# Decode attention with gate over sum applied to its outputs, and fifteen loads moved to ACT's queue

## Chip, core and metric

One core of a Trainium2 chip runs the whole step in one launch. The metric is device time in microseconds. TensorE is called PE below, VectorE DVE, ScalarE ACT, GpSimd POOL and SyncE SP; SP issues most of the DMAs and does no arithmetic.

## What is computed

One inference step of a decoder layer, on 1024 prompt positions and on 8 decode sequences of 4 new positions each, all in float32. The input projection gives queries, keys and values of three attention branches, a retention group and gates; attention and retention feed the output projection, and a convolutional feed-forward network (FFN) follows. What the change touches is the attention of the decode sequences, three softmaxes whose outputs are summed by gates:

```python
s_c = jnp.einsum('bqgrd,bcgd->bgrqc', qg, kc) * scale
p_c = jnp.where(m_c, jax.nn.softmax(jnp.where(m_c, s_c, NEG), axis=-1), 0.0)
o_cmp = jnp.einsum('bgrqc,bcgd->bqgrd', p_c, vc)
...
p_s = jax.nn.softmax(s_s, axis=-1).reshape(B, NSA_KV, NSA_REP, Qn, k_top, SEL_BLOCK)
o_sel = jnp.einsum('bgrqkl,bgqkld->bqgrd', p_s, vs)
...
p_w = jax.nn.softmax(jnp.where(m_w, s_w, NEG), axis=-1)
o_win = jnp.einsum('bgrqw,bwgd->bqgrd', p_w, vw.astype(F32))
out = g[..., 0:1] * o_cmp + g[..., 1:2] * o_sel + g[..., 2:3] * o_win
```

The keys and values of the selected branch come from a paged cache: 8 pages of 128 rows for each sequence, gathered by a page table.

## The kernel before

**Stages.** The input projection runs over six groups of weight columns; the decode caches' compressed keys are made beside the first four. `run(4, ...)` projects the attention queries and `run(5, ...)` the retention gates (`ret_gate`, a Silu on ACT at L299); the decode attention (`decode_phase`) runs beside both, as a generator that `run` advances by a few steps for each row tile. In the trace `run(5, ...)` lies at about 340 to 411 us. Then comes the prompt's attention (to 860), with the rest of the decode attention in its first 140 us, the output projection woven into it, and the FFN (888 to the end).

**Weights.** Each weight column group comes in four slices of 512 KB (`w_raw(u)`, u = 0 to 23). A slice lands in one of two raw buffers, `RAW[u % 2]`, and `w_split(u)` turns it into a high and a low part: `wh` by ACT (L186) and `wl` by DVE (L187). The load of slice u + 2 is issued when slice u is split. A projection takes three matmuls for each pair of slice part and row tile (L235, L237, L238; L240 for the decode rows), on `xt` and `xa`, the row tiles' high and low parts.

**Decode attention.** Four rounds, B = 0 to 3, of two sequences each. A round first computes the compressed branch (L709 is its exp, L718 and L722 two small matmuls that rank the blocks), then the window branch (keys `gw`, 512 wide) and then the selected branch (pages `ga`, 1024 wide). `probabilities` (L742) makes a softmax: two exps on ACT (L748: 64 x 512 or 64 x 1024, and 64 x 32 for the new keys) with their sums, the sum's reciprocal times the gate on DVE (L749 to L751), and both blocks of exps multiplied by that on DVE (L753). PE transposes the result (L763), ACT copies it out of PSUM (L764), and PE multiplies it with the values (L779 pages or window, L786 new keys, L784 compressed keys) into one bank, `XB`. The window branch's sum waits in `of` until the selected branch's is added to it.

**Pages.** `load_page` reads a page number into a register of SP and issues the page's load (L463, 128 KB). `run` calls it up to `PG` = 3 times for each row tile; the selected branch issues what is left over.

**Prompt keys and values.** `load_kv` reads the prompt's keys (4 loads of 256 KB, into the two raw buffers) and later its values (4 loads, into `VT`) back from the output in HBM. They, the masks' constants (`hn`, `fin`, `cmpm`) and the last weights are issued by SP (`D` is SP's queue, `S` is ACT, `V` DVE, `T` PE, `G` POOL).

**Order.** A scheduler sets the order on each engine when the kernel is built, by the dependences and priorities of the code; the decode generator's steps have a raised priority. Each engine works its list in order, and so does each queue.

```python
def probabilities(src, n, z, gate):
    s, r, m = [sc[:, 8 + y:9 + y] for y in range(2)], sc[:, 10:11], sc[:, 11:12]
    V.tensor_reduce(m, NM[:, 0:z + 1], AX.X, ALU.min)
    for y, (o, a) in enumerate(((P[:64, 0:n], src), (pn, pn))):
        S.activation(o, a, AF.Exp, bias=m, accum_out=s[y])
```

Of the kernel before, what the change touches and what calls it, by code (L numbers as in the profile page):

```python
# [11 lines left out]
ALU = mybir.AluOpType  # L12
# [47 lines left out]
def hymba(ctx: ExitStack, tc: tile.TileContext, A, O):  # L60
# [99 lines left out]
    def w_raw(u, ks=(0, 2)):  # L160

        c, q = divmod(u, 4)
        if u < 24:
            n = CH_N[c]
            o = 8 * CH_OFF[c] + q * 2 * n
            a, b = ks[0] * n, ks[1] * n
            D.dma_start(raw_ap(u)[:, a:b], A["w_in"][:, o + a:o + b])

    def raw_ap(u):
        return (RAW[u % 2] if u not in (2, 3) else QBIG[:, 1024 + u * 1024:2048 + u * 1024])[:, 0:2 * CH_N[u // 4]]  # L170
# [452 lines left out]
    def decode_phase():  # L623
# [14 lines left out]
            return DCT[:p, o:o + s]  # L638

        of = QBIG[:64, 4608:4736]  # L640
        pc = QBIG[:64, 5120:5248]
        pct, pn = sm[:, 0:64], sm[:, 64:96]
        imr, im, eq, dn = sm[:, 96:113], sm[:, 113:130], sm[:, 130:144], sm[:, 144:160]
        grow = sm[:, 176:188].rearrange("p (b c) -> p b c", c=3)
# [56 lines left out]
        def compressed(B):  # L701

            scc = t_bank()[:64, 0:64]
            for b in range(2):
                scores(scc, KCD[:, B * 128 + b * 64:B * 128 + b * 64 + 64], b)
            nm, s1, r1 = sc[:, 0:1], sc[:, 1:2], sc[:, 2:3]
            V.tensor_reduce(nm, scc[:, 0:63], AX.X, ALU.max, negate=True)
            V.memset(pc[:, 63:64], 0.0)
            S.activation(pc[:, 0:63], scc[:, 0:63], AF.Exp, bias=nm, accum_out=s1)  # L709
            V.reciprocal(r1, s1)  # L710
            V.tensor_scalar(pc[:, 0:63], pc[:, 0:63], r1, None, ALU.mult)
            yield
            tb = t_bank()
            T.transpose(tb[0:64, 0:64], pc[:, 0:64], ident[:64, :64])
            V.tensor_copy(pct, tb[0:64, 0:64])
            yield
            tb = t_bank()
            T.matmul(tb[0:64, 0:17], pct, dc("ovl"), start=True, stop=True)  # L718
            V.tensor_copy(imr, tb[0:64, 0:17])
            yield  # L720
            tb = t_bank()
            T.matmul(tb[0:64, 0:17], dc("rsum"), imr, start=True, stop=True)  # L722
            V.tensor_copy(im, tb[0:64, 0:17])
            mn, mx = sc[:, 3:4], sc[:, 4:5]
            jv = dc("jv")
            V.tensor_reduce(mn, im[:, 1:15], AX.X, ALU.min)
            V.scalar_tensor_tensor(eq, im[:, 1:15], mn, jv[:, 1:15], ALU.is_equal, ALU.mult)
            V.tensor_reduce(mx, eq, AX.X, ALU.max)
            V.tensor_scalar(dn, jv, mx, NEG, ALU.is_equal, ALU.mult)
            V.tensor_scalar(pc[:, 0:64], pc[:, 0:64], grow[:, B, 0:1], None, ALU.mult)  # L730
            V.tensor_copy(pc[:, 64:128], pc[:, 0:64])
            yield

        NM = sc[:, 5:8]
# [7 lines left out]

        def probabilities(src, n, z, gate):

            s, r, m = [sc[:, 8 + y:9 + y] for y in range(2)], sc[:, 10:11], sc[:, 11:12]
            V.tensor_reduce(m, NM[:, 0:z + 1], AX.X, ALU.min)
            for y, (o, a) in enumerate(((P[:64, 0:n], src), (pn, pn))):
                S.activation(o, a, AF.Exp, bias=m, accum_out=s[y])  # L748
            V.tensor_tensor(s[0], s[0], s[1], ALU.add)  # L749
            V.reciprocal(r, s[0])  # L750
            V.tensor_tensor(r, r, gate, ALU.mult)  # L751
            for a in (P[:64, 0:n], pn):
                V.tensor_scalar(a, a, r, None, ALU.mult)  # L753

        def key_scores(src, b):

# [14 lines left out]
        def out(b):  # L771
            return XB[32 * b:32 * b + 32, 0:128]
# [7 lines left out]

        def last_values(br, B):
            for b in range(2):
                if not br:
                    T.matmul(out(b), PD[:, 9, b], VCD[:, B], start=False, stop=False)  # L784
            for b in range(2):
                T.matmul(out(b), PD[0:32, 8, b], VN[:, br], start=False, stop=True)  # L786

        def window_branch(B):
            gw = [GW[:, b * 1024:(b + 1) * 1024] for b in range(2)]
# [10 lines left out]
            last_values(1, B)  # L800
            window(B + 1)
            yield
            V.tensor_copy(of, XB[:64, 0:128])

        def selected_branch(B):
            while pages:
# [11 lines left out]
            yield  # L818
            yield from transposed(8)
            tb = t_bank()[:, 0:64]  # L820
            T.transpose(tb, pc, ident[:64, :64])
            for b in range(2):
                q = slice(64 * b, 64 * b + 64)
                V.tensor_copy(PD[q, 9, b], tb[q, b * 32:(b + 1) * 32])
# [1 line left out]
            for hf in range(2):  # L826
# [3 lines left out]
                    for b in range(2):  # L830
                        gather(B + 1, b)
                yield
            V.tensor_tensor(of, XB[:64, 0:128], of, ALU.add)
            tb = t_bank()[:, 0:64]
            T.transpose(tb, of, ident[:64, :64])
            for z in range(2):
# [112 lines left out]
    pr.release()  # L949
    side = decode_phase()  # L950
    next(side)
    run(4, q_proj, staged, down, side, SB[0], 3)
    KT = pa_.tile([128, 8 * HALF], F32R, name="kt", tag="a0")[:, 0:4096].rearrange("p (b g t) -> p b g t", b=2, g=2)
    VT = []
# [3 lines left out]
    def load_kv():  # L958

        src = O["kv"][0:1024, 256:768].rearrange("(i p) (b z c) -> p i b z c", p=128, b=2, z=2)  # L960
        for y in range(2):
            for b in range(2):
                if VT:
                    D.dma_start(VT[0][:, 4 * y:4 * y + 4, b], src[:, 4 * y:4 * y + 4, b, 1])
                else:
                    D.dma_start(RAW[y].rearrange("p (i b c) -> p i b c", i=4, b=2)[:, :, b], src[:, 4 * y:4 * y + 4, b, 0])

    def masks():
        lt["a"] = kcv.tile([128, 352], F32R, name="ma", tag="ws1")
# [16 lines left out]
    def building(f, order):  # L986

        for z, i in enumerate(order):
            f(i, i == order[-1])
            if z == 1:  # L990
                section("MC", HN[:, 0:MC.size])
                load_kv()
            elif z == 3:
                masks()
# [181 lines left out]
    lt["mo"] = mk(p2, "mo", 128, F32R)  # L1176
    lt["cmpm"] = mk(p2, "cmpm", 120)
    o, _ = SECT["MC"]
    D.dma_start(FIN[:, 0:128], A["const"][:, o + 128:o + 256])
    D.dma_start(lt["cmpm"], A["const"][:, o + 256:o + 376])  # L1180
    V.tensor_copy(lt["mo"], FIN[:, 0:128])
    del ring[:]

# [666 lines left out]
```

## Time and profile before

| what | us |
|---|---|
| median of 3 runs | 1547.77 (1543.68 to 1548.29) |
| profiled execution, its own time | 1553.57 |
| its span, first to last instruction | 1551.8 |
| PE busy in the span | 1488.8 (96%) |
| DVE, ACT, POOL busy | 981.9, 649.8, 617.1 |
| mean TensorE clock granted | 0.976 of full speed |

The trace is that of the profiled execution, so its own time is the one to set sums against. A row of PE's list gives start, length and instruction, and in brackets how long PE had been idle before it and what ended the wait. The clock column of a stretch is the granted TensorE clock as a share of 2.4 GHz: 0.50 is the lower level, 1.2 GHz, and 0.57 is a stretch that is mostly there. Matmuls overlap, so their spacing tells more than their length.

### The profile page before, as it was taken

To read this page: it belongs to the slowest core of one execution; us is meant where nothing else is said; L and a number is where in the kernel's file an instruction comes from. 1 tells how busy PE (TensorE), PEld (TensorE's weight loads), DVE (VectorE), ACT (ScalarE), POOL (GpSimd) and SP (SyncE) were. 2 spreads that over 40 slices of the span, in tenths; PEclk is the share of its full clock that TensorE was granted. 3 is DMA by queue.
4 is the path that set the end of the run, shared out by engine and by line. 5 is a ranking of instruction groups with operands and counts; after the bars stand their busy time and mean duration, and the time that the engine had idled before them with its cause. 6 is when DMAs were issued, how large, how long until landed. Compare 5 with 4: busy or idle time off the path is not lost.

```text
span 1551.8 us, 28741 instructions
## 1 busy us (share of the span) xinstructions
PE 1488.8 (96%) x10722; PEld 1306.8 (84%) x10722; DVE 981.9 (63%) x1831; ACT 649.8 (42%) x1417; POOL 617.1 (40%) x789
## 2 busy tenths in 40 slices
PE   7999999989999789999999899999999999999998
PEld 5898877757656568787877899999999999999998
DVE  6876525364567664645567888777778777644531
ACT  6464324124445554455445433333333334544430
POOL 3453311350224464545345233333333333544552
PEclk8999999998999899999999899999999999999999
DMA  7452301163431100100002124555554535887662
GB/s 265 145 171 63 96 4 55 31 202 95 149 99 59 55 15 28 31 29 28 28 28 69 65 104 156 163 164 167 172 178 165 170 117 168 274 258 220 206 199 66
DMA packets 129568, 184.54 MB, mean 119 GB/s; under 512 B 20356, under 2 KB 89092, under 8 KB 129428
## 3 DMA queue, kind: packets, MB, share of 16 engines
q1 hardware_dynamic: 127940, 178.08, 36.2%
q0 software_dynamic: 1488, 4.63, 0.9%
q8 instruction: 84, 1.38, 0.4%
q14 instruction: 56, 0.46, 0.1%
HBM read 132.84 MB, written 49.82 MB: 118 GB/s over the span
## 4 chain that ended last, share of the span: by engine, by line
PE 82%; DVE 7%; issue 4%; DMA 2%; POOL 2%; ACT 2%; SPq 1%; DVEq 0%; ACTq 0%; POOLq 0%
PE PS L466 51%; PE PS L235 6%; PE PS L238 5%; PE PS L237 5%; PE PS L1103 3%; PE PS L1241 2%; PE PS L1240 2%; PE PS L1242 2%; POOL pwin L1091 1%; PE PS L779 1%; DVE live L1077 1%; DMA raw<-in_w_in 1%; DVE pt L1109 1%; DMA rbig<-in_xT 1%; PE PS L240 1%
## 5 line engine op out<-in xcount | busy, mean ns | idle before, releaser
L466 PE MATMUL PS<-x,wop 128*128 128x264 f32 x3696 | 457.7, 287 | 7.2 <-ACT wop L122 2.9
L466 PEld LDWEIGHTS PS<-x,wop 128*128 128x128 f32 x3696 | 455.7, 190 | 8.9 <-ACT wop L122 3.1
L466 PE MATMUL PS<-h,wop 128*128 128x264 f32 x1848 | 225.6, 285 | 0.0
L466 PEld LDWEIGHTS PS<-h,wop 128*128 128x128 f32 x1848 | 225.4, 188 | 0.0
L123 POOL TENSOR_TENSOR wop<-sp,wop 128x512 fp32r<-128x512 f32 (+1 forms) x105 | 140.0, 1339 | 182.4 <-ACT wop L122 169.1
L122 ACT ACTIVATE wop<-sp 128x512 fp32r<-128x512 f32 x150 | 90.1, 608 | 205.5 <-PE PS L466 105.4
L123 POOL TENSOR_TENSOR wop<-rawf,wop 128x512 fp32r<-128x512 f32 x42 | 70.9, 1689 | 124.3 <-ACT wop L122 124.2
L1077 DVE TENSOR_REDUCE live<-PS 128x1 f32<-128x640 f32 (+5 forms) x112 | 72.0, 652 | 59.8 <-PE PS L466 47.4
L466 PE MATMUL PS<-kt,qt 128*128 128x320 f32 (+5 forms) x400 | 102.0, 351 | 4.8 <-ACT vt L1079 3.9
L1085 POOL TENSOR_TENSOR live<-live 128x2 f32<-128x2 f32 (+1 forms) x64 | 14.5, 227 | 226.2 <-DVE live L1084 203.8
L235 PE MATMUL PS<-wh,xt 128*128 128x512 f32 (+1 forms) x240 | 94.3, 394 | 10.2 <-ACT xt L122 7.3
L466 PE MATMUL PS<-pt,vt 128*64 128x256 f32 x528 | 80.8, 413 | 6.2 <-DVE pt L1109 4.3
L1109 DVE COPY pt<-PS 128x512 f32<-128x512 f32 (+1 forms) x99 | 66.9, 685 | 30.7 <-PE PS L1103 28.4
L1079 ACT ACTIVATE pwin<-PS,live 128x64 f32<-128x64 f32 (+5 forms) x128 | 61.5, 485 | 58.7 <-DVE live L1077 41.9
L1091 POOL TENSOR_TENSOR pwin<-pwin,live 128x64 f32<-128x64 f32 (+5 forms) x128 | 79.1, 649 | 2.2
L238 PE MATMUL PS<-wh,xt 128*128 128x512 f32 (+1 forms) x192 | 75.3, 393 | 2.8 <-DVE xt L123 2.8
L1240 PE MATMUL PS<-mix,wo 128*128 128x256 f32 (+1 forms) x256 | 75.9, 297 | 1.2 <-ACT mix L122 1.1
L123 DVE TENSOR_TENSOR h<-rawf,h 128x528 fp32r<-128x528 f32 x51 | 44.5, 880 | 51.0 <-ACT h L122 50.7
L235 PE MATMUL PS<-wh,xa 128*128 128x512 f32 (+1 forms) x192 | 75.3, 393 | 1.0 <-ACT qbig L253 0.5
L237 PE MATMUL PS<-wl,xt 128*128 128x512 f32 (+1 forms) x192 | 75.5, 394 | 0.0
L466 PEld LDWEIGHTS PS<-kt,qt 128*128 128x128 f32 x400 | 63.7, 197 | 13.1 <-ACT vt L1079 5.1
L1241 PE MATMUL PS<-mix,wo 128*128 128x256 f32 (+1 forms) x256 | 74.1, 290 | 0.5 <-DVE mix L123 0.5
(388 smaller groups left out, 3082.0 us busy)
## 6 DMA issues: line engine op xcount, KB each, us to landing
rawf<-in_w_ffn_in SPq DMA_DIRECT2D x30, 512.0 KB, 3.3
rawf<-scr_x SPq DMA_DIRECT2D x51, 264.0 KB, 3.5
scr_x<-rbig SPq DMA_DIRECT2D x44, 264.0 KB, 2.6
ws<-in_w_ffn_out SPq DMA_DIRECT2D x64, 176.0 KB, 3.0
scr_s<-ws SPq DMA_DIRECT2D x64, 176.0 KB, 2.2
scr_x<-qbig SPq DMA_DIRECT2D x33, 264.0 KB, 2.1
raw<-in_w_in SPq DMA_DIRECT2D x17, 512.0 KB, 3.6
ga<-in_cache_sel SPq DMA_DIRECT2D x64, 128.0 KB, 2.1
```

The lines of the kernel that those rows point to most:

```text
L122: a = S.activation(h, src, AF.Copy)
L123: return a.ins, (eng or V).tensor_tensor(l, src, b32(h), ALU.subtract).ins
L235: T.matmul(ps, xh(i, kk), wh[:, k], start=first, stop=False)
L237: T.matmul(ps, xh(i, kk), wl[:, k], start=False, stop=False)
L238: T.matmul(ps, xl(i, kk), wh[:, k], start=False, stop=end)
L466: T.matmul(o, a, b, start=start, stop=stop, skip_group_check=True)
L1077: V.tensor_reduce(nm, src, AX.XY, ALU.max, negate=True)
L1079: S.activation(d.rearrange("p (b c) -> p b c", b=src.shape[1]), src, AF.Exp, bias=nm, accum_out=st9[:, 12 + e + g:13 + e + g])
L1091: G.tensor_tensor(x, x, f.to_broadcast([128, x.shape[1]]), ALU.mult)
L1109: V.tensor_copy(pt[0:n], tb)
L1240: T.matmul(o, wh, MIX[:, 0, k, 0:n], start=k == 0, stop=False)
L1241: T.matmul(o, wh, MIX[:, 1, k, 0:n], start=False, stop=False)
```

## The change

1. `probabilities` no longer scales the exps. The sum of the two exp sums is made on ACT, its reciprocal on DVE, and ACT multiplies it by the gate into a column of its own, `f`. The transposes take the unscaled exps. The outputs are scaled when they are read from `XB`: the window branch by a multiplication in place of a copy, the selected branch by a multiply-and-add in place of an addition.
2. The compressed branch, whose probabilities keep their gate, gets columns 128 to 255 of `XB` to itself and one more DVE addition (64 x 128). Its gate is multiplied, and its block doubled, by one ACT instruction (`pc2`) instead of two of DVE.
3. The four weight loads from u = 20 on, the eight key and value loads and three constants are issued by ACT.
4. From `run(4, ...)` on, `PG` is 4.

```diff
-            D.dma_start(raw_ap(u)[:, a:b], A["w_in"][:, o + a:o + b])
+            (S if u >= 20 else D).dma_start(raw_ap(u)[:, a:b], A["w_in"][:, o + a:o + b])
...
-        pc = QBIG[:64, 5120:5248]
+        pc, pc2 = QBIG[:64, 5120:5184], QBIG[:64, 4736:4864]
...
-            V.tensor_scalar(pc[:, 0:64], pc[:, 0:64], grow[:, B, 0:1], None, ALU.mult)
-            V.tensor_copy(pc[:, 64:128], pc[:, 0:64])
+            S.activation(pc2.rearrange("p (b c) -> p b c", b=2), pc.unsqueeze(1).to_broadcast([64, 2, 64]), AF.Copy, scale=grow[:, B, 0:1])
...
-            s, r, m = [sc[:, 8 + y:9 + y] for y in range(2)], sc[:, 10:11], sc[:, 11:12]
+            s, m = [sc[:, 8 + y:9 + y] for y in range(2)], sc[:, 11:12]
+            r, f = sc[:, 10:11], sc[:, 12 + z:13 + z]
...
-            V.tensor_tensor(s[0], s[0], s[1], ALU.add)
-            V.reciprocal(r, s[0])
-            V.tensor_tensor(r, r, gate, ALU.mult)
-            for a in (P[:64, 0:n], pn):
-                V.tensor_scalar(a, a, r, None, ALU.mult)
+            S.activation(r, s[0], AF.Identity, bias=s[1])
+            V.reciprocal(r, r)
+            S.activation(f, r, AF.Copy, scale=gate)
...
             for b in range(2):
-                if not br:
-                    T.matmul(out(b), PD[:, 9, b], VCD[:, B], start=False, stop=False)
-            for b in range(2):
                 T.matmul(out(b), PD[0:32, 8, b], VN[:, br], start=False, stop=True)
+            for b in range(0 if br else 2):
+                T.matmul(XB[32 * b:32 * b + 32, 128:256], PD[:, 9, b], VCD[:, B], start=True, stop=True)
...
-            V.tensor_copy(of, XB[:64, 0:128])
+            V.tensor_scalar(of, XB[:64, 0:128], sc[:, 13:14], None, ALU.mult)
...
-            V.tensor_tensor(of, XB[:64, 0:128], of, ALU.add)
+            V.scalar_tensor_tensor(of, XB[:64, 0:128], sc[:, 14:15], of, ALU.mult, ALU.add)
+            V.tensor_tensor(of, XB[:64, 128:256], of, ALU.add)
...
+    PG = 4
     run(4, q_proj, staged, down, side, SB[0], 3)
...
-                    D.dma_start(VT[0][:, 4 * y:4 * y + 4, b], src[:, 4 * y:4 * y + 4, b, 1])
+                    S.dma_start(VT[0][:, 4 * y:4 * y + 4, b], src[:, 4 * y:4 * y + 4, b, 1])
...
-                    D.dma_start(RAW[y].rearrange("p (i b c) -> p i b c", i=4, b=2)[:, :, b], src[:, 4 * y:4 * y + 4, b, 0])
+                    S.dma_start(RAW[y].rearrange("p (i b c) -> p i b c", i=4, b=2)[:, :, b], src[:, 4 * y:4 * y + 4, b, 0])
...
-                section("MC", HN[:, 0:MC.size])
+                o, n = SECT["MC"]
+                S.dma_start(HN[:, 0:n], A["const"][:, o:o + n])
...
-    D.dma_start(FIN[:, 0:128], A["const"][:, o + 128:o + 256])
-    D.dma_start(lt["cmpm"], A["const"][:, o + 256:o + 376])
+    S.dma_start(FIN[:, 0:128], A["const"][:, o + 128:o + 256])
+    S.dma_start(lt["cmpm"], A["const"][:, o + 256:o + 376])
```

The scheduler puts the instructions in another order as well. Line numbers of the changed kernel are one to two lower in `decode_phase` (L761, L762, L765, L777, L781 are L763, L764, L767, L779, L786 of before). Three places follow; DVE has 39 rows fewer in all, ACT 32 more, and two of ACT's are table loads.

**First, the last weight slice** (raw_107 here, u = 23). SP's queue at the end of the first round's pages, before and then after; `gw` and `out_kw` are the window rows' load and copy:

```order
L463 DMA ga_3060<-in_cache_sel 128x256
L462 TENSOR_LOAD ixd
L462 ISA x2
L167 DMA raw_107<-in_w_in 128x1024
L966 DMA raw_106<-out_kv 128x4x128
L664 DMA out_kw<-gw 128x2x1024
```

```order
L463 DMA ga_3060<-in_cache_sel 128x256
L462 TENSOR_LOAD ixd
L462 ISA x2
L664 DMA out_kw<-gw 128x2x1024
L463 ISA
L463 DMA ga_3059<-in_cache_sel 128x256
```

The weight load and the key loads have left SP, and the next round's pages (ga_3059) follow at once. ACT, at the splits of the two slices ahead, before and then after:

```order
L676 ACTIVATE vn<-pdp 32x256
L186 ACTIVATE wh_97<-raw_107,ict 128x512 x2
L186 ACTIVATE wh_98<-raw_106,ict 128x512 x2
L253 ACTIVATE qbig<-PS,live 128x512
L709 ACTIVATE qbig,dsm<-PS,dsm 64x63
L254 ACTIVATE PS<-qbig 128x512 x2
```

```order
L676 ACTIVATE vn<-pdp 32x256
L186 ACTIVATE wh_97<-raw_107,ict 128x512 x2
L186 ACTIVATE wh_98<-raw_106,ict 128x512 x2
L167 DMA raw_107<-in_w_in 128x1024
L253 ACTIVATE qbig<-PS,live 128x512
L965 DMA raw_106<-out_kv 128x4x128
L709 ACTIVATE qbig,dsm<-PS,dsm 64x63
L254 ACTIVATE PS<-qbig 128x512
L965 DMA raw_106<-out_kv 128x4x128
```

The load stands right behind the splits, and two key loads stand between the activations that follow.

**Second, PE where `run(5, ...)` begins.** wh_99 and wl_104 are the last slice's parts; L763 (now L761) transposes the window branch's exps, the L685 rows with `ga` are the page scores. Before, and then after:

```order
L763 MATMUL PS<-pers,pdp 128x64 x4
L718 MATMUL PS<-dct,dsm 64x17
L767 MATMUL PS<-pers,dsm 32x64
L779 MATMUL PS<-gw,ptd 32x128 x8
L722 MATMUL PS<-dsm,dct 64x17
L685 MATMUL PS<-kn,qb 32x32 x2
L786 MATMUL PS<-vn,ptd 32x128 x2
L690 MATMUL PS<-pers,qbig 128x32 x4
L685 MATMUL PS<-ga_3060,qb 32x512
L685 MATMUL PS<-ga_3059,qb 32x512
```

```order
L235 MATMUL PS<-wh_99,xt_95 128x512
L235 MATMUL PS<-wh_99,xa_89 128x512
L240 MATMUL PS<-wl_104,xt_95 128x512
L235 MATMUL PS<-wh_99,xt_95 128x512
L237 MATMUL PS<-wl_104,xa_89 128x512
L238 MATMUL PS<-wh_99,xa_89 128x512
L235 MATMUL PS<-wh_99,xa_89 128x512
L761 MATMUL PS<-pers,pdp 128x64 x4
L240 MATMUL PS<-wl_104,xt_95 128x512
L237 MATMUL PS<-wl_104,xa_89 128x512
```

Both pieces stand behind the same row. Before, the four page scores (two pairs) come ahead of all matmuls of the last slice; now the slice's matmuls come first, 19 projection rows stand between the window branch and the first pair of page scores, and 22 more between the two pairs.

**Third, PE where the projections end and the prompt's attention begins.** `xt_91` is the last row tile, L1025 transposes the first attention block's queries, the L466 rows are attention scores. From the second round's L722 on before, and from its L761 on now:

```order
L722 MATMUL PS<-dsm,dct 64x17
L767 MATMUL PS<-pers,dsm 32x64
L779 MATMUL PS<-gw,ptd 32x128 x8
L979 MATMUL PS<-pers,raw_107 128x128 x2
L235 MATMUL PS<-wh_99,xt_92 128x512
L237 MATMUL PS<-wl_104,xt_92 128x512
L238 MATMUL PS<-wh_99,xt_92 128x512
L466 MATMUL PS<-ma 128x128 x2
L235 MATMUL PS<-wh_96,xt_91 128x512
L237 MATMUL PS<-wl_101,xt_91 128x512
L238 MATMUL PS<-wh_96,xt_91 128x512
```

```order
L238 MATMUL PS<-wh_99,xt_91 128x512
L761 MATMUL PS<-pers,pdp 128x64 x4
L718 MATMUL PS<-dct,dsm 64x17
L722 MATMUL PS<-dsm,dct 64x17
L978 MATMUL PS<-pers,raw_107 128x128 x2
L765 MATMUL PS<-pers,dsm 32x64
L777 MATMUL PS<-gw,ptd 32x128 x8
L781 MATMUL PS<-vn,ptd 32x128 x2
L1025 MATMUL PS<-pers,qbig 128x128 x2
L685 MATMUL PS<-ga_3060,qb 32x512
L685 MATMUL PS<-ga_3059,qb 32x512
L466 MATMUL PS<-ma 128x128
```

Before, L1025 stands three rows further down, with 19 projection matmuls behind it; now the last projection is the first row shown, and the window branch's steps and L1025 come behind it.

## Rows read from the trace of the kernel before

**Rows 1.** The page: busy time by engine, and the chain that ended last by engine.

```profile
PE 1488.8 (96%) x10722; PEld 1306.8 (84%) x10722; DVE 981.9 (63%) x1831; ACT 649.8 (42%) x1417; POOL 617.1 (40%) x789
...
PE 82%; DVE 7%; issue 4%; DMA 2%; POOL 2%; ACT 2%; SPq 1%; DVEq 0%; ACTq 0%; POOLq 0%
```

**Rows 2.** Stretches: length, busy us of PE, PEld, DVE, ACT, POOL; PE clock, DMA share, GB/s.

```profile
341.00:361.00 20.00, 12.05 (x29) 7.25 (x28) 9.34 (x26) 6.12 (x11) 0.05 (x1) 0.57 0.65 208
...
411.00:500.00 89.00, 80.71 (x575) 52.74 (x574) 59.65 (x164) 46.20 (x156) 35.40 (x61) 0.92 0.30 95
500.00:550.00 50.00, 40.07 (x230) 24.48 (x229) 34.63 (x60) 24.40 (x51) 27.10 (x23) 0.83 0.14 43
1073.00:1300.00 227.00, 227.00 (x1858) 227.00 (x1859) 178.35 (x237) 78.99 (x111) 84.62 (x122) 1.00 0.49 160
```

**Rows 3.** PE's instructions, 346 to 362: start, us, instruction, [idle before, releaser].

```profile
346.07 1.92 PE L685 MATMUL PS<-ga,qb 128*32 128x512 f32 x4 [4.67 <-DMA ga<-in_cache_sel]
...
350.86 0.80 PE L235 MATMUL PS<-wh,xt 128*128 128x512 f32 x1 [2.86 <-ACT wh L186]
351.45 0.63 PE L235 MATMUL PS<-wh,xa 128*128 128x512 f32 x1
351.88 0.63 PE L240 MATMUL PS<-wl,xt 128*128 128x512 f32 x1
...
356.20 0.79 PE L235 MATMUL PS<-wh,xa 128*128 128x512 f32 x1 [0.42 <-DVE hn L246]
...
361.70 0.39 PE L235 MATMUL PS<-wh,xa 128*128 128x512 f32 x1
361.93 0.40 PE L237 MATMUL PS<-wl,xa 128*128 128x512 f32 x1
```

**Rows 4.** SP's queue, 327 to 354: start, us the group took, DMA and count.

```profile
327.44 12.39 SPq L463 DMA_DIRECT2D ga<-in_cache_sel  x11
...
343.59 0.34 SPq L167 DMA_DIRECT2D raw<-in_w_in  x1
...
345.55 8.24 SPq L966 DMA_DIRECT2D raw<-out_kv  x3
```

**Rows 5.** ACT's instructions, 323 to 358.

```profile
323.17 2.55 ACT L186 ACTIVATE wh<-raw,ict 128x512 fp32r<-128x512 f32 x4
...
350.08 1.33 ACT L186 ACTIVATE wh<-raw,ict 128x512 fp32r<-128x512 f32 x2 [11.97 <-DMA raw<-in_w_in]
...
355.46 1.28 ACT L299 ACT_TABLE_LOAD   x1
356.75 0.66 ACT L299 ACTIVATE PS<-PS,live 128x512 f32<-128x512 f32 x1
```

**Rows 6.** Stretches again: 330 to 335, while the pages are issued.

```profile
330.00:335.00 5.00, 5.00 (x25) 3.18 (x25) 3.73 (x13) 1.68 (x5) 4.81 (x4) 1.00 0.46 138
```

**Rows 7.** PE and DVE at the query of the first attention block, 402 to 408.

```profile
402.74 0.44 PE L1025 MATMUL PS<-pers,qbig 128*128 128x128 f32 x2
...
406.64 0.43 DVE L123 TENSOR_TENSOR qt<-PS,qt 64x256 fp32r<-64x256 f32 x1 [0.44 <-ACT qt L122]
```

**Rows 8.** ACT, DVE, POOL and PE at the fourth round's selected softmax, 512 to 519.

```profile
512.54 0.30 ACT L748 ACTIVATE dsm<-dsm 64x32 f32<-64x32 f32 x1
...
513.35 1.83 DVE L751 TENSOR_TENSOR dsm<-dsm 64x1 f32<-64x1 f32 x1
515.21 2.35 DVE L753 TENSOR_SCALAR pdp<-pdp,dsm 64x1024 f32<-64x1024 f32 x1
...
513.27 3.75 POOL L1091 TENSOR_TENSOR psel<-psel,live 128x1024 f32<-128x1024 f32 x2
...
517.62 1.11 PE L763 MATMUL PS<-pers,pdp 64*128 64x64 f32 x8 [3.33 <-DVE pdp L753]
```

**Rows 9.** Stretches again: behind the third round's window softmax, and behind rows 8.

```profile
448.00:456.00 8.00, 6.89 (x41) 4.51 (x41) 4.95 (x18) 3.21 (x10) 5.46 (x10) 0.57 0.01 2
517.00:525.00 8.00, 7.28 (x50) 5.15 (x50) 1.88 (x5) 2.04 (x6) 0.02 (x1) 0.57 0.00 0
```

More of the change, by code (lines that the diff above doesn't have):

```diff
@@ L820, in selected_branch @@
             tb = t_bank()[:, 0:64]
-            T.transpose(tb, pc, ident[:64, :64])
+            T.transpose(tb, pc2, ident[:64, :64])
             for b in range(2):
```

## The prediction

> **What bounds the kernel now.** First the page's head and chain [rows 1]: TensorE (PE) is busy 1488.8 of 1551.8 us, and the chain that ended last is 82% PE. A change therefore gains only where PE waits, or where it works at the lower clock after a wait. Second the table by stretches [rows 2]: the feed-forward part has nothing to give (227.00 of 227.00 us busy at clock 1.00). What PE loses near the changed lines lies in three stretches: 341 to 361 (12.05 of 20 us busy, clock 0.57), 411 to 500 (8.3 us idle, 0.92) and 500 to 550 (9.9 us idle, 0.83). Third the instructions of PE in the first stretch [rows 3], beside SP's queue [rows 4] and ACT [rows 5] for who is late; last the softmax of the fourth decode round [rows 8] and the stretches behind two softmaxes [rows 9].
>
> **Part 1: who issues the last weights (gain).** PE waits three times in [rows 3]: 4.67 us for cache pages, 2.86 us for the split of the last weight slice (ACT L186), 0.42 us for DVE: 7.95 us. While it waits the clock falls from 2.4 to 1.2 GHz: projection matmuls start 0.43 us apart at 351.45 and 0.23 us apart at 361.70. The low clock ends near 360.2; the 9.35 us of work from 350.86 to there would take 9.35 x 0.23 / 0.43 = 5.0, so it costs 4.3 us, and of the page scores' 1.92 us at 346.07 about 0.9. Together 13.2 us.
> The cause is SP's order. ACT split the slices before by 325.72 [rows 5], and their raw buffers were free, but the load of the last slice was issued at 343.59 [rows 4], behind the round's pages, eleven of which held SP for 12.39 us (1.13 each); it landed 6.47 us later (350.08 on ACT, [rows 5]). In the changed order it stands on ACT right behind those splits, so it is issued near 327. Even if it takes twice as long as here it is there by 340. The transfers have room: in 330 to 335 the 16 DMA engines are busy 0.46 [rows 6]. And PE now finds that slice's matmuls ahead of the window branch's transposes, and the page scores in two pairs behind 29 and 51 projection matmuls, 6.7 and 11.7 us at 0.23 each; the pages need only keep their present pace, and SP's queue is shorter by the loads it gave away. So I take both waits as gone. What is late next: the first Silu (L299) now comes just behind the window softmax, and its table load of 1.28 us [rows 5] has less to hide under; I charge 1.2 us. Part 1: 13.2 - 1.2 = 12.0 us, bounds 4 (only the weight's wait and its share of the clock, 2.86 + 1) and 13.2.
> The load takes 1.28 us in [rows 5], from 355.46, and Silu begins at 356.75, so nothing is added behind it. The Trainium skill (ScalarE: Activation LUTs, What ACT_TABLE_LOAD costs) counts 2.66 us for a switch, 1.28 of load and 1.38 of drain; the trace shows the first alone, and by the page the sum would end 1.4 us later.
> Fifteen DMAs become ACT's: four weight loads, eight key and value loads, three constants. What issuing costs ACT no row of before shows, as ACT issues none. From below 0; from above SP's 0.34 us for the weight load [rows 4], 15 x 0.34 = 5.1 us of ACT while ACT is busy 6.12 of 20 us and 46.20 of 89 [rows 2]; hidden, so I take 0 on PE's path. If the cover is gone (a wait at such a DMA, with exp and Silu queued behind), see the third rival.
>
> **Part 2: the end of the projections (loss).** The third piece of the order shows what now stands behind PE's last projection: the second round's window branch and the query transposes, with no projection between. In the kernel before, the same query (L1025 at 402.74) had its evictions, passed back and forth between ACT and DVE, until 407.07 [rows 7] underneath projection matmuls. From the end of L1025 (403.18) that is 3.9 us, of which the page scores that now stand behind it cover about 0.5; that leaves 3.4 exposed. The transposes' eviction and the block ranking ahead of it may add 1. On the other side, the present start of attention has waits of its own (part of the 8.3 us in 411 to 500), some of which this pause absorbs. I take -3.5 us; bounds -8 (a second 3 us of low clock like those in [rows 9], and the 1 above) and 0.
>
> **Part 3: probabilities no longer scaled (gain).** Removed per softmax: the sum, the gate's product and two scalings on DVE, 8 softmaxes; added: two one-column ACT instructions, at most the 0.30 us of the 64x32 exp [rows 8] each, which nothing waits for until the output is read, and one DVE addition of 64x128 per round, under the 0.43 us of a 64x256 [rows 7], 1.7 us for all four beside other work. The compressed branch trades two DVE instructions for one on ACT; its value matmuls go to columns of their own in the same number. From the query projection on, four pages go out per step of the loop where three did, which only makes them earlier. All this I take at 0, hidden by the projections or by other rounds' work. What it takes off PE's path: the transposes wait for exp alone. In the fourth round exp ended near 512.9, but DVE's two instructions behind it took 1.83 and 2.35 us (the first ended with the first of POOL's two passes over psel, the second 0.5 us behind the other, 3.75 us both), and PE waited 3.33 us [rows 8]. The stretch behind, 517 to 525, ran at 0.57: 7.28 us of work that needs 4.15 at full clock, 3.1 us lost [rows 9]. Sum 6.4. What is late next is that psel of POOL, ready at 517.02: PE reaches it some 1 us too early. So 5.4. In the third round's window (448 to 456) idle and clock together cost 1.1 + 6.89 x 0.43 = 4.1 us [rows 9]; DVE's queue there loses about a microsecond of work ahead of the reductions that PE waits for; half, 2.0. Part 3: 7.4 us, bounds 1 and 16 (all the idle time of 500 to 550 and both clock losses, 9.9 + 3.1 + 3.0).
>
> **Sum.** The profiled execution took 1553.57 us. 1553.6 - 12.0 + 3.5 - 7.4 = 1537.7. It lies 5.8 above the median of the runs, 1547.77, so 1531.9 against the median: 1532, 1.0% less. Everything behind 550 keeps its order and PE stays the bound there, so the shift reaches the end whole.
>
> **Rivals.**
> 1. The pages decide again: the moved loads share the DMA engines with them, and at 345.55 three loads held SP 8.24 us [rows 4]. Then the 4.67 us and most of the low clock stay, part 1 is worth 4: 1540. For it: the engines are that busy when loads bunch. Against: 0.46 in 330 to 335.
> 2. The scaling was hidden: other waits on POOL and on exp end just behind, part 3 is worth 1: 1538. For it: the psel row; against: seven of the softmaxes and the 3.33 us row itself.
> 3. Slower: ACT stands at its DMAs. A load waits in order until earlier transfers that share its counter have landed; three key loads held SP 8.24 us, 2.75 each [rows 4]. Eight such on ACT, with exp, Silu and key evictions behind them, cost 22 us if PE's banks run out each time: 1532 + 22 = 1554. It decides from 20 us on (the 15.9 of the sum and the 4.6 of the bound below). Against: the pages whose landing they wait for are issued well before.
> 4. Only issue time is saved: the weight load goes no earlier in effect, and SP loses 15 x 0.34 = 5.1 us of queue, so part 1 is worth 5: 1539. The Trainium skill has it as a rule (DMA: Bandwidth & Descriptors, Issuing engines are not separate DMA queues): DMAs of several engines run on the same 16 DMA engines, and spreading them only saves the issuing time, usually small. Here eleven pages hold SP 12.39 us, which is not small, so the trace speaks for part 1.
> 5. Better: no low clock remains between 411 and 550, part 3 near its upper bound, 16: 1523.
>
> **Chances.** Forecast 0.50 (its own range 1526 to 1538), rival 1 0.14, 2 0.15, 3 0.07, 4 0.06, 5 0.08. A measurement of this kernel can tell about 0.3%, 4.6 us, from no change: faster is under 1543.1, slower over 1552.4. The four rivals near 1540 could each lose another 4 to 5 us by part 2's lower bound; a quarter of their weight and some of the forecast's goes to "same". Faster 0.80, same 0.13, slower 0.07. The range, 1522 to 1546, holds all but the slower case and the tail of "same".
>
> **What would show it.** Right: the last weight load issued by ACT before 330; no wait above 1 us before its matmuls nor before the page scores; clock near 1.0 from 341 to 361; a pause of 3 to 4 us before the first scores of attention, released by the query's evictions; the fourth round's transposes released by exp. Wrong: on ACT, exp or Silu idle behind a DMA; PE waiting for pages again; 500 to 550 as idle as before.

## The result and the profile after

The changed kernel took 1535.97 us in the median (1533.75 to 1540.20, 6 runs), the kernel before 1547.66 (1543.68 to 1550.49, 6 runs): 11.7 us less. The ratio is 0.9933, with an interval of 0.9916 to 0.9950. Measured a second time, it was 0.9931 (0.9907 to 0.9956). The forecast was 1532, in a range of 1522 to 1546.

The profiled execution took 1536.39 us, 17.2 less than the profiled one of before; the sum of the prediction for that one was 1537.7. So the sum held, within 1.3 us, for the execution it was made from, and the median moved by less. Why is the main question below.

The page of the kernel after, its busy time by engine and its DMA queues (packets, MB, share of 16 engines):

```profile
PE 1478.0 (96%) x10722; PEld 1299.8 (85%) x10722; DVE 970.4 (63%) x1795; ACT 658.3 (43%) x1439; POOL 615.0 (40%) x789
...
q1 hardware_dynamic: 122708, 173.57, 35.7%
q10 hardware_dynamic: 5232, 4.51, 1.0%
```

Against [rows 1] DVE lost 11.5 us of work, ACT gained 8.5, and the moved loads appear as a queue of their own, q10. Now the stretches, with the columns of [rows 2]: where the last weights used to be late, then three of 4 us behind the end of the projections, then a middle piece of the FFN.

```profile
341.00:361.00 20.00, 19.56 (x105) 13.95 (x100) 9.02 (x30) 6.99 (x14) 0.00 (x0) 1.00 0.41 141
404.00:408.00 4.00, 0.92 (x7) 0.60 (x6) 2.55 (x5) 3.96 (x11) 0.03 (x1) 1.00 1.05 388
408.00:412.00 4.00, 3.94 (x27) 3.16 (x28) 1.68 (x7) 3.68 (x15) 3.84 (x6) 0.54 0.05 19
412.00:416.00 4.00, 4.00 (x28) 3.32 (x25) 1.31 (x2) 0.78 (x2) 3.26 (x6) 0.61 0.33 99
...
880.00:1056.00 176.00, 176.00 (x1442) 175.94 (x1441) 141.29 (x186) 62.33 (x87) 65.93 (x98) 1.00 0.47 153
```

The 20 us that had 12.05 us of PE at clock 0.57 now have 19.56 at 1.00. Behind the end of the projections stands a new pause: 0.92 us of PE in 4, and then 8 us mostly at the low clock (0.54 and 0.61). The FFN is full, as before.

ACT's queue and ACT, near the last weight slice (the rows that answer to [rows 4] and [rows 5]):

```profile
327.44 0.33 ACTq L167 DMA_DIRECT2D raw<-in_w_in  x1
...
330.11 0.61 ACTq L965 DMA_DIRECT2D raw<-out_kv  x1
...
330.33 1.29 ACT L254 ACTIVATE PS<-qbig 128x512 f32<-128x512 f32 x2
...
333.41 1.34 ACT L186 ACTIVATE wh<-raw,ict 128x512 fp32r<-128x512 f32 x2
```

The load is issued at 327.44 where it was 343.59, and the slice is split at 333.41 where it was 350.08. PE's matmuls that need it, at 337.36, wait for nothing.

The fourth round's selected softmax, on PE, ACT, DVE and POOL (the rows that answer to [rows 8]):

```profile
503.57 0.71 PE L761 MATMUL PS<-pers,pdp 64*128 64x64 f32 x8
...
502.24 1.15 ACT L748 ACTIVATE pdp<-pdp,dsm 64x1024 f32<-64x1024 f32 x1 [0.18 <-DVE dsm L746]
...
504.15 0.16 DVE L750 RECIPROCAL dsm<-dsm 64x1 f32<-64x1 f32 x1 [0.38 <-ACT dsm L749]
...
501.25 3.75 POOL L1091 TENSOR_TENSOR vt<-vt,live 128x1024 f32<-128x1024 f32 x2
```

The stretches behind them, to set against 517 to 525 of [rows 9]:

```profile
505.00:510.00 5.00, 5.00 (x55) 3.92 (x52) 1.26 (x3) 1.68 (x5) 3.89 (x3) 1.00 0.01 3
510.00:516.00 6.00, 6.00 (x45) 3.82 (x43) 4.51 (x9) 4.30 (x6) 1.14 (x1) 1.00 0.00 0
```

The transposes start 0.2 us behind the end of the 64 x 1024 exp, with no wait; the 3.33 us of before are gone, and so is the low clock behind them (505 to 516 at 1.00).

### The profile page after: what moved, and what is told of

It is laid out like the page before. It is cut to its first block, busy times and chain, and to the rows that moved or that the text cites. A ratio compares the mean times of both kernels' runs of the same rounds, so it can differ in the third digit from the quotient of the medians.

```text
span 1534.6 us, 28716 instructions
## 1 busy us (share of the span) xinstructions
PE 1478.0 (96%) x10722; PEld 1299.8 (85%) x10722; DVE 970.4 (63%) x1795; ACT 658.3 (43%) x1439; POOL 615.0 (40%) x789
## 4 chain that ended last, share of the span: by engine, by line
PE 83%; DVE 7%; issue 3%; DMA 2%; ACT 2%; POOL 2%; SPq 0%; DVEq 0%; ACTq 0%; POOLq 0%
PE PS L466 52%; PE PS L235 6%; PE PS L238 5%; PE PS L237 5%; PE PS L1103 3%; PE PS L1241 2%; PE PS L1240 2%; PE PS L1242 2%; DVE live L1077 1%; POOL pwin L1091 1%; PE PS L777 1%; DMA raw<-in_w_in 1%; PE PS L240 1%; DMA qbig<-in_w_in 0%; PE PS L685 0%
## 5 line engine op out<-in xcount | busy, mean ns | idle before, releaser
L466 PE MATMUL PS<-x,wop 128*128 128x264 f32 x3696 | 456.8, 286 | 9.5 <-ACT x L122 4.2
L466 PEld LDWEIGHTS PS<-x,wop 128*128 128x128 f32 x3696 | 454.4, 189 | 11.5 <-ACT x L122 4.6
L466 PE MATMUL PS<-h,wop 128*128 128x264 f32 x1848 | 225.6, 285 | 0.0
L466 PEld LDWEIGHTS PS<-h,wop 128*128 128x128 f32 x1848 | 225.4, 188 | 0.0
L466 PE MATMUL PS<-kt,qt 128*128 128x320 f32 (+5 forms) x400 | 103.3, 354 | 7.1 <-ACT vt L1079 5.1
L466 PE MATMUL PS<-pt,vt 128*64 128x256 f32 x528 | 78.4, 403 | 6.1 <-DVE pt L1109 4.9
L466 PEld LDWEIGHTS PS<-kt,qt 128*128 128x128 f32 x400 | 64.3, 198 | 16.9 <-ACT vt L1079 5.8
```

Source lines behind the costliest of these rows:

```text
L466: T.matmul(o, a, b, start=start, stop=stop, skip_group_check=True)
```

## A measure for the stretches

To compare kernels whose order differs I use one sum. The loss of a window is its length less PE's busy time multiplied by the granted clock; work is that product. The losses of windows of 2 us, from the trace by stretches, are added up, and the span is cut where a kernel has done the same amount of work: at 320 us of work (ahead of the last weights), 360, 400 (behind the pause at the end of the projections), 430 (behind the third round's window softmax), 520 and 1400. One example: 404 to 408 above gives 4 - 0.92 x 1.00 = 3.08. All profiles, in us of loss:

| kernel (own time of the profiled execution) | last weights, 320 to 360 | end of projections, 360 to 400 | third round's window softmax, 400 to 430 | rest of rounds three and four, 430 to 520 | 520 to 1400 |
|---|---|---|---|---|---|
| before (1553.57) | 13.6 | 5.7 | 6.6 | 23.1 | 24.6 |
| before, second profile (1554.02) | 13.4 | 5.7 | 6.5 | 23.0 | 25.1 |
| before, third profile (1545.41) | 9.4 | 6.3 | 6.7 | 20.0 | 22.0 |
| weights on ACT (1541.98) | 3.5 | 6.1 | 6.1 | 22.0 | 23.9 |
| all loads on ACT (1546.94) | 1.3 | 6.0 | 6.1 | 23.8 | 26.4 |
| weights early on SP (1540.39) | 1.1 | 7.2 | 6.2 | 21.6 | 23.4 |
| softmax only (1540.72) | 12.0 | 5.7 | 2.3 | 15.4 | 26.5 |
| weights back on SP (1538.74) | 9.5 | 8.4 | 1.3 | 15.7 | 22.7 |
| after (1536.39) | 0.4 | 9.0 | 3.2 | 18.2 | 23.0 |
| after, second profile (1537.41) | 0.4 | 8.8 | 4.8 | 16.1 | 24.3 |
| softmax, weights early on SP, table early (1539.32) | 1.6 | 10.0 | 2.5 | 17.3 | 22.7 |
| after, table early (1536.26) | 0.5 | 7.6 | 4.8 | 16.0 | 24.6 |
| after, table early, again (1540.07) | 0.5 | 7.2 | 3.2 | 17.8 | 25.7 |
| after, slower decode pace (1541.39) | 0.5 | 7.8 | 1.8 | 21.8 | 27.5 |

Each line is one execution. Ahead of 320, where the edits change little, the three profiles of the kernel before lose 16.7, 14.1 and 14.8 us, and behind 520 they differ by 3: a difference of one or two us between two single lines says little.

## The experiments

**The kernel before, a second and a third profile.** No edit.

> The kernel before, unchanged, profiled a second time, to find which stretch made its first profiled execution 5.8 us longer than the median. Theory A (the waits behind the late weight load are fixed by SP's order): 341 to 361 loses 13 us again, within 1, and the 5.8 us lie in the stretches at the low clock between 411 and 550, which come and go. Theory B (the late weights and pages depend on the DMA engines' traffic): 341 to 361 loses some 8 us in this execution and the sum of the prediction was too large there. The time against itself: ratio 1.000, within 0.003.

Measured: 1548.22 us against 1549.07, ratio 0.9998 (0.9979 to 1.0017). Its twelve runs go from 1542.49 to 1554.08 us, and the granted clock goes with them: 0.986 in the shortest, 0.977 in the longest. This profile is again of a long execution, with the same loss at the last weights; so theory A held as far as it went, but it could not say what an execution of usual length loses.

> A third profile of the kernel before, for the spread of its executions (1542 to 1554 us). If this one is near 1548 or below, its loss by stretch shows which of the stretches is the shorter: the last weights and pages (13.5 us in both profiles so far) or the ends of the softmaxes between 411 and 550. Expected from the granted clocks: the former stays at 13, the latter lose 4 to 6 us less.

Measured: 1545.41 us. Against the expectation, 4 us of the difference lie at the last weights (9.4 against 13.4), which is the size that theory B had given them, and only 3 us in the third and fourth rounds (20.0 against 23). The stretch from 341 to 361 in the second profile, the same in the third, and PE and ACT there in the third:

```profile
341.00:361.00 20.00, 12.26 (x32) 7.65 (x31) 9.43 (x26) 6.13 (x11) 0.00 (x1) 0.57 0.62 207
```

```profile
341.00:361.00 20.00, 14.10 (x51) 8.46 (x48) 9.89 (x28) 6.78 (x13) 0.61 (x1) 0.74 0.65 214
```

```profile
346.74 1.92 PE L685 MATMUL PS<-ga,qb 128*32 128x512 f32 x4 [5.00 <-DMA ga<-in_cache_sel]
...
349.07 0.79 PE L235 MATMUL PS<-wh,xt 128*128 128x512 f32 x1 [0.41 <-ACT wh L186]
...
348.29 1.33 ACT L186 ACTIVATE wh<-raw,ict 128x512 fp32r<-128x512 f32 x2 [9.86 <-DMA raw<-in_w_in]
```

The wait for pages is as long (5.00 us), but the weight load, issued at 344.09, is in by 348.29, 4.2 us later instead of 6.47, so the second wait is 0.41 us instead of 2.86, and the low clock ends some 5 us sooner.

**The weights alone on ACT's queue.**

```diff
-            D.dma_start(raw_ap(u)[:, a:b], A["w_in"][:, o + a:o + b])
+            (S if u >= 20 else D).dma_start(raw_ap(u)[:, a:b], A["w_in"][:, o + a:o + b])
```

> The kernel before with one edit: the four last weight loads issued by ACT; softmax, key and value loads, constants and pages per step as before. Theory (part 1 and part 2 of the prediction belong to this edit alone): no wait above 1 us between 337 and 361 and clock 1.00 there, 12 us gained; the window branch and the query transposes stand behind the last projection, 3 to 4 us lost; in all 8 us (ratio 0.995, and 0.997 if the usual execution loses less there than the profiled one). Rival (only issue time is saved): under 2 us, ratio above 0.998, page scores still waiting.

Measured: 1544.02 us, ratio 0.9974 (0.9958 to 0.9989): 4.0 us, half of the 8 that were expected, and near the 0.997 that the expectation gave for a usual execution which loses less there. The mechanism is there: no wait for pages or weights. The first stretch still loses 3.5 us, by a wait of 1.0 us for a DVE copy (L824) and the clock behind it. And the end of the projections, which I had expected to lose 3 to 4 us more, loses 6.1 us where the kernel before loses 5.7 to 6.3.

**All fifteen loads on ACT's queue, softmax as before.** The edit is every `D` to `S` of the change.

> The kernel before with all fifteen DMAs issued by ACT, and nothing else. Theory (the other eleven are hidden): the same as with the weights alone within 1.5 us. Rival (ACT stands at its DMAs): 3 us or more slower than with the weights alone, with exp, Silu or key evictions of ACT idle behind a DMA.

Measured: 1544.10 us, ratio 0.9968 (0.9951 to 0.9985), the same as with the weights alone. No exp or Silu of ACT was found idle behind a DMA between 325 and 412; only one split of weights waited 2.0 us for its own load. ACT's queue took 0.33 to 0.61 us for an issue while ACT itself went on computing (330.11 and 330.33 in the changed kernel's rows above). The rival that ACT stands at its DMAs is out.

**The softmax edits alone.** The changed kernel with every moved load back on SP and `PG` 3.

> The changed kernel with all DMAs back on SP's queue and three pages per step: the softmax edits alone. Theory: 341 to 361 as in the kernel before (8 us of waits at the low clock after), the fourth round's transposes released by exp, stretch 500 to 550 some 6 us shorter and the third round 2: 7 us in all, ratio 0.9955. Rival (the scaling was hidden): within 1 us, ratio above 0.999, the 3.3 us wait replaced by one for POOL's psel.

Measured: 1539.82 us, ratio 0.9949 (0.9933 to 0.9965): 7.9 us. From 430 to 520 it loses 15.4 us where before loses 20.0 to 23.1, and at the third round's window softmax 2.3 where before loses 6.5 to 6.7, twice the 2 us that were expected there. The end of the projections is as before (5.7). PE's waits from 395 to 430, in total, times and longest:

```profile
PE PS L466 <- DVE ma L1126: 2.3, 1, 2.3
PE PS L1101 <- ACT pwin L1077: 0.2, 1, 0.2
```

**The changed kernel again, and with its weights back on SP's queue.** The first has no edit; the second is `(S if u >= 20 else D)` back to `D`.

> The changed kernel, unchanged, on the chip and in the hour of the next three, and profiled a second time. Theory: ratio to the kernel before 0.9933 within 0.0015; of its loss by stretch, nothing again at the last weights and the page scores, and again some 12 us around the end of the projections (2.9 us of wait behind exp on ACT, and the low clock after it). Rival (the pause there was one execution's accident): under 8 us.

Measured: 1537.68 us, ratio 0.9931; the pause behind the projections is there again, with 8.8 us lost in its stretch (before: 5.7 to 6.3). The 12 us of the expectation are this and the third round's window softmax together. Its waits from 388 to 412, the two longest:

```profile
PE PS L466 <- ACT vt L1079: 2.9, 1, 2.9
PE PS L685 <- DVE pdp L811: 1.1, 1, 1.1
```

> The changed kernel with its four weight loads back on SP's queue; key and value loads, constants, four pages per step and the softmax edits stay. Theory (of the fifteen loads only the last weights matter): page scores and last weights wait again as in the kernel before, 12 us lost there in the profiled execution, and the softmax gain stays; ratio to before 0.995, as with the softmax edits alone, 3 us slower than the changed kernel. Rival (the eleven other loads gave SP the time): no wait for pages, ratio 0.993 as the changed kernel.

Measured: 1538.74 us, ratio 0.9945 (0.9930 to 0.9960), some 2 us slower than the changed kernel (0.9933, 0.9931), with intervals that overlap. PE's two longest waits from 336 to 362, the page scores and the last weights:

```profile
PE PS L685 <- issue: 5.2, 1, 5.2
PE PS L235 <- ACT wh L186: 0.9, 1, 0.9
```

The first stretch loses 9.5 us (12 had been expected). So of the fifteen loads it is the weights that decide these two waits, and they are worth 9 us where they stand; but the stretches from 360 to 520 lose 8.4, 1.3 and 15.7 us here, against 9.0, 3.2 and 18.2 (8.8, 4.8 and 16.1 in the second profile) in the changed kernel.

**The weights early, on SP's own queue.** The kernel before with

```diff
+            with tc.high_priority(offset=3000) if u >= 22 else ExitStack():
+                D.dma_start(raw_ap(u)[:, a:b], A["w_in"][:, o + a:o + b])
```

> The kernel before with one edit: the last two weight loads keep SP's queue but get a raised priority, so that they are issued ahead of most of the pages. Theory (the place in the order is what counts, not whose queue it is): no wait of PE for the last weights or the pages, the same ratio as with the weights on ACT, 0.9974 within 0.0015. Rival (SP's time is what counts): the pages are as late as before, a wait for them of 3 us or more stays, ratio above 0.999.

Measured: 1540.17 us, ratio 0.9944 (0.9924 to 0.9963): 8.7 us, no slower than with the weights on ACT, and faster than the 0.9974 within 0.0015 that was expected. SP's queue, and PE from 341 to 361:

```profile
326.71 0.42 SPq L168 DMA_DIRECT2D raw<-in_w_in  x1
328.25 15.26 SPq L464 DMA_DIRECT2D ga<-in_cache_sel  x13
```

```profile
341.00:361.00 20.00, 19.12 (x95) 13.27 (x90) 9.33 (x29) 6.01 (x12) 0.00 (x0) 1.00 0.59 190
```

The last load goes out at 326.71, ahead of thirteen pages that hold SP 15.26 us, and PE waits for neither, since the scheduler has put the scores behind the projections. So an earlier place in the order is enough to end both waits; it takes no second queue. Whether the second queue costs or gives a few us beside that, these two kernels do not tell.

**The exp table loaded early.** The changed kernel with one line behind the constants' loads:

```diff
+    S.activation(FIN[:, 511:512], ident[:, 0:1], AF.Exp)
```

> The changed kernel with one ACT instruction more, an exp of one column right behind the constants' loads at the end of the projections, so that the exp table is loaded in an idle stretch of ACT. Theory (what is exposed at the end of the projections is a chain through ACT: table load 1.28, exp 1.15 + 0.3, then the first attention exp): the 2.9 us wait falls to 1.6 and, if the pause no longer drops the clock, 3 us more are gained: 1.3 to 4.5 us faster than the changed kernel. Rival (DVE's reductions of 2.4 us bind, the table load lies beside them): no change, the wait moves to DVE.

> The changed kernel with the exp table loaded early, a second time, since 3 us are not much beside the spread of the runs. Theory: ratio to before 0.991 within 0.0015 again, and the low clock behind the end of the projections shorter than in the changed kernel (12 us lost there in both of its profiles). Rival (the first time was luck): 0.993 or above, as the changed kernel.

Measured: 1534.70 us and ratio 0.9911 (0.9889 to 0.9932) the first time, 1538.33 and 0.9938 (0.9918 to 0.9957) the second, on another chip. The waits at the end of the projections, the first time and the second:

```profile
PE PS L466 <- ACT vt L1079: 1.8, 2, 1.6
PE PS L466 <- ACT qt L122: 1.1, 1, 1.1
```

```profile
PE PS L466 <- ACT vt L1079: 1.4, 2, 1.3
PE PS L466 <- ACT qt L122: 1.1, 1, 1.1
```

The wait behind the chain on ACT fell from 2.9 to 1.6 and 1.3 us, as the theory has it, while the wait for the query ahead of it grew from 0.5 to 1.1. The stretch loses 7.6 and 7.2 us in place of 9.0 and 8.8, so the table load was part of this pause. The second ratio is what the rival of that run had given, though: whether the kernel as a whole is faster is not settled by the two, and nothing here is shown to beat the changed kernel.

**A slower decode pace.** The changed kernel with `SB = (2.5, 0.8)` instead of `(2.5, 1)`.

> The changed kernel with 0.8 decode steps per row tile beside the last projection instead of 1; on PE the transposes of the first queries then stand 14 rows ahead of the last projection, the second round's window branch still behind it. Theory (the query's evictions are the exposed part): 3 to 4 us faster than the changed kernel. Rival (the softmax of the selected branch ahead of the first attention exp is what binds): within 1 us of it, with the wait behind ACT or DVE still there.

Measured: 1538.39 us, ratio 0.9927 (0.9906 to 0.9948), no different from the changed kernel, as the rival had it. PE's waits from 388 to 412:

```profile
PE PS L761 <- DVE kt L983: 1.8, 1, 1.8
PE PS L765 <- ACT ptd L762: 0.4, 1, 0.4
PE PS L466 <- ACT vt L1079: 0.4, 1, 0.4
```

The wait behind ACT's exps has shrunk from 2.9 to 0.4 us, but the transposes of the window branch now wait 1.8 us, behind DVE's key copies. The end of the projections loses 7.8 us in place of 9.0 and 8.8 and the third round's window softmax 1.8 in place of 3.2 and 4.8, but 430 to 520 loses 21.8 in place of 18.2 and 16.1. The steps that no longer stand at the end of the projections stand later.

**Softmax edits, weights early on SP, table early, no load on ACT.**

> What helped, together, without the move of loads to ACT: the softmax edits, the last two weight loads ahead of the pages on SP's own queue by a raised priority, and the exp table loaded early. Theory (the terms add): softmax 8, weights 4 to 8, table 2 to 3 us faster than before, 14 to 18 us, ratio 0.989 to 0.991, no slower than the changed kernel with the table early. Rival (ACT's queue is needed, as SP's pages come later with the weights ahead of them): a wait for pages or a ratio of 0.993 and above.

Measured: 1539.26 us, ratio 0.9943 (0.9929 to 0.9958): 8.8 us, not the 14 to 18 that the terms would add up to. No wait for pages came back (1.6 us lost in the first stretch), so the ratio is the rival's but its reason is not there. The end of the projections loses 10.0 us, the most of all profiles. So the gains do not add even where ACT issues nothing.

## Why the prediction was right in sign and range, and 4 us too large

**Part 1, the last weights.** The mechanism was right in each step: the load issued near 327, the slice there by 334, both waits gone, clock 1.00. The charge of 1.2 us for Silu's table load was too much; PE waits 0.2 us there. The size was too large for the usual execution, as far as the profiles show. 13.2 us came from a profiled execution of 1553.57 us, and two profiles of such long ones (13.6, 13.4) agree, but in one of 1545.41 us the same place loses 9.4, and in the two later kernels whose last weights still come late, 12.0 and 9.5. In the execution of 1545.41 us the last weight load lands in 4.2 us and not in 6.47, so one of the two waits is nearly absent. The step that failed is the conversion: I took 5.8 us off the end and left each term at its size in the long execution. The terms themselves are what was long.

**Part 2, the end of the projections.** A pause of the forecast place and size came: 2.9 us, 1.0, and smaller ones, with 8 us at the low clock behind. Its releaser was another than the one I named. The query's evictions cost 0.5 us; what binds is ACT, where the selected softmax of the second round stands ahead of the first exp of the prompt's attention. ACT in the changed kernel, and PE's wait for it:

```profile
403.38 1.28 ACT L748 ACT_TABLE_LOAD   x1 [1.73 <-DVE dsm L746]
404.68 1.15 ACT L748 ACTIVATE pdp<-pdp,dsm 64x1024 f32<-64x1024 f32 x1
...
406.25 0.69 ACT L1079 ACTIVATE vt<-PS,live 128x512 f32<-128x512 f32 x1
...
407.08 0.50 PE L466 MATMUL PS<-kt,qt 128*128 128x256 f32 x2 [2.92 <-ACT vt L1079]
```

As a difference between before and after the pause cost about what was forecast: 9.0 and 8.8 us lost from 360 to 400 against 5.7 to 6.3, so 2.5 to 3.3 us where the prediction had 3.5. That the size agrees is luck, since it was worked out from the query's evictions, and the path that binds is another. The kernel before pauses there as well, for other reasons: its two longest waits of PE from 411 to 425 are

```profile
PE PS L1103 <- POOL psel L1091: 1.1, 1, 1.1
PE PS L690 <- ACT psel L1079: 0.6, 1, 0.6
```

What makes the pause longer is shown in part. With the exp table loaded early the wait behind ACT is 1.3 and 1.6 us shorter and the stretch loses 1.2 to 1.8 us less, about the 1.28 us of the load. With the softmax edits alone, where the window branch stands under the last projections, the stretch loses 5.7 us; with early weights alone, where it stands behind them, 6.0 to 7.2; with both 8.8 and 9.0 in the changed kernel and 10.0 with the weights early on SP. But with the weights back on SP's queue, where the window branch is under the projections again, it loses 8.4. So, as far as single profiles tell, neither edit alone brings the longer pause, and it does not hang on the early weights alone. Whether four pages per step or the key and value loads on ACT have a part in it was not tried by itself.

**Part 3, the softmax.** 7.4 us were forecast and 7.9 measured for the edits alone. The 3.33 us wait and the low clock behind it are gone. At the third round's window softmax 2.0 us were forecast, and the loss fell by 4.3 with the edits alone and by 1.7 to 3.5 in the changed kernel. The 1 us that I charged for psel did not come: PE reaches it at 509.72, behind POOL's second pass. The Trainium skill has a reason for the long DVE rows (SBUF — State Buffer, Who interferes with whom): a DVE instruction with two SBUF inputs, or one of the tensor_scalar kind in its two-port mode, contends with GpSimd for a pair of ports, which whoever comes first keeps for its whole instruction, and a DVE instruction with one SBUF input outside that mode does not. [rows 8] agree, with 1.83 and 2.35 us beside POOL's passes, and so does the kernel after, where the reciprocal takes 0.16 us beside one.

**The sum.** Against the forecast's 15.7 (1547.77 to 1532) the kernel gained 11.7 in the medians, 10.4 by the ratio. By single edits the shortfall can't be shared out. Softmax alone 7.9 us and weights on ACT alone 4.0 make 11.9, which looks as if the two simply added; but softmax alone 7.9 and weights early on SP alone 8.7 make 16.6, and together, with the table early, they measured 8.8. By stretches it can, as far as single profiles go. From the first profile of before to the two of after the terms come out near the forecast: 13.2 for the last weights, 3.3 and 3.1 lost at the end of the projections, 3.4 and 1.8 at the third round's window softmax, 4.9 and 7.0 from 430 to 520 (forecast 12.0, 3.5, 2.0 and 5.4). From the third profile, the one nearest the median, they are 9.0, 2.7 and 2.5 lost, 3.5 and 1.9, 1.8 and 3.9: 11.6 and 12.3 us in all. So what the forecast had too much lies in the two places where the long executions lose more than the third: 3 us at the last weights and 1.5 to 3.6 from 430 to 520. This is as good as single profiles are: the third execution and the two of after differ by 9.0 and 8.0 us as a whole, since the changed kernel's two lose 1.0 and 2.3 us more behind 520, and the first of them 1.9 more ahead of 320 (16.7 against 14.8).

**The rivals.** Pages that decide again, a scaling that was hidden and an ACT that stands at its DMAs are ruled out by the runs above. "Only issue time is saved" failed by its mechanism, as the waits went altogether. The rule of the Trainium skill that I set beside it (DMA: Bandwidth & Descriptors, Issuing engines are not separate DMA queues) agrees with the runs, though: a second queue gave nothing that a better place in the first did not (0.9944 on SP, 0.9974 on ACT). The better case, in which no low clock remains, did not come: 408 to 416 stands at 0.54 and 0.61.

**What stays open.** Weights on ACT and weights early on SP give the same order on PE, and their times, 1544.02 and 1540.17 us, were measured on different chips; the intervals just overlap. I cannot say whether the 1.0 us wait and its low clock in the former's profile are usual. What makes the late weight load land in 4.2 or in 6.5 us, and what makes one execution of the same kernel longer than another, was not tried.

## What to carry to other kernels

A sum made from one profiled execution has the terms of that execution. Where runs of one kernel spread over 12 us, take a second and a third profile before pricing a stall, and price it by the one nearest the median. The late transfer here was late by its place in a queue, and a better place was enough; try the place before another queue. Two edits that each move the same side work under or out from under a main loop need not add; look where the steps that one of them frees come to stand. And cut a measure of loss where the terms of the sum are cut, so that a gain in one place does not hide a loss in the next.

## What the runs showed of the hardware that I had not expected

The spread of the kernel before, 1542.49 to 1554.08 us in twelve runs, goes with its mean granted clock, 0.986 to 0.977: nine thousandths of 1550 us are 14 us. The two go together; which is the cause isn't shown.

Waits of the same size can come with several microseconds at 1.2 GHz behind them, or without. The stretch of the third round's window softmax, in the first and in the second profile of the changed kernel:

```profile
438.00:440.00 2.00, 1.35 (x11) 0.98 (x10) 2.00 (x7) 2.00 (x8) 0.00 (x0) 1.00 0.00 0
440.00:442.00 2.00, 1.38 (x11) 0.86 (x10) 1.48 (x7) 1.20 (x7) 0.54 (x3) 1.00 0.00 0
442.00:444.00 2.00, 2.00 (x17) 1.22 (x16) 0.17 (x1) 0.82 (x2) 2.00 (x3) 1.00 0.02 4
```

```profile
438.00:440.00 2.00, 1.33 (x11) 1.01 (x11) 1.93 (x7) 2.00 (x9) 0.07 (x1) 1.00 0.00 0
440.00:442.00 2.00, 1.38 (x10) 0.98 (x8) 1.63 (x7) 1.29 (x6) 0.39 (x3) 0.89 0.00 0
442.00:444.00 2.00, 2.00 (x13) 1.17 (x13) 0.00 (x0) 0.98 (x2) 2.00 (x3) 0.50 0.02 4
```

PE was idle for 1.27 us of 438 to 442 in the first and for 1.29 in the second; the granted clock stayed at 1.00 in the first and was 0.50 in 442 to 444 of the second.

DMAs issued by ACT cost its arithmetic nothing that the traces show: the queue's 0.33 to 0.61 us for an issue can lie beside ACT's own instructions (330.11 and 330.33 above), and eleven more such loads changed nothing (1544.02 and 1544.10 us).
